# Up projection by Strassen's product, up and down as two stages

## The chip, the cores and the metric

One Trainium2 chip, one of its cores. The metric is device time of one execution in microseconds. The engines are named as in the profile: PE (TensorE; PEld are its weight loads), DVE (VectorE), ACT (ScalarE), POOL (GpSimd) and SP, which here only issues DMA transfers.

## What is computed

One decoder layer over 1024 tokens of width 1024 in float32: attention and a gated DeltaNet side by side, an MLP, a gated embedding and a last norm. The change is in the MLP:

```python
h = h + jnp.concatenate([attn_out, dn_out], axis=-1) @ w_o[i]
m = rmsnorm(h, norm_mlp[i])                                   # 1024 x 1024
h = h + jnp.square(jax.nn.relu(m @ w_up[i])) @ w_down[i]      # w_up 1024 x 4096, w_down 4096 x 1024
gate = jax.nn.sigmoid(rmsnorm(h, norm_ple[i]) @ w_ple_gate[i])
```

## The kernel before

Everything is kept transposed: channels lie on the 128 partitions, tokens in columns, in two halves `hb` of 512 tokens. `hT(hb, j)` is the piece of h for channels 128 j to 128 j + 127 and half hb.

Each float32 operand is split in two numbers of the PE's rounded type: `split` makes the high part on ACT (L219, a cast) and the low part on DVE or POOL (L220, source minus high part). `mm3` (L232) then takes three matmuls per product: high x high, high x low, low x high. A matmul has a 128x128 weight piece and 512 tokens.

The rows 1/rms of the norm don't enter the operand: `norm_M` makes M = h x gain alone (L1237 and L1238), `rows_M` squares and sums h, takes the power -0.5 on POOL (`rstd`, L1252), and spreads the row over all partitions by two matmuls with ones (`dg`, `row_bc`). The result `rB[hb]` multiplies the relu's argument when a bank of PSUM is read (`relu2`, L1288), ACT squares it (L1289), and it is split into `aT`.

The MLP is one loop over 8 values of c, 512 of the 4096 inner channels each. Up: two halves mp of 256 columns, four loads of weights each (`wunit2`: 2 k tiles x 256 columns, 256 KB), 8 k tiles, two token halves, two column pieces, three passes. Down, for the same c right behind it: two halves nh of 512 output columns, two token halves, 4 k tiles, 4 column pieces, three passes; the four banks are added to h by DVE (L1339). The first up products use banks and an order of their own, because the last group of w_out (`w_out(1)`, banks named bk_6732 and bk_6733 below) still runs then. After the loop come the gate weights `WG` and the last loop over token tiles.

The program is recorded in Python order, and a scheduler then fixes the order on every engine; each engine works through its own list in that order and waits at an instruction whose inputs are not there. Transfers of one queue are issued in order too. Tiles come from pools with a fixed number of buffers: `wraw` 2 (loaded weights), `wsp` 4 (split weights), `cvp` 2.

Of the kernel before, what the change touches and what calls it, by code (L numbers as in the profile page):

```python
# [18 lines left out]
P = 128  # L19
# [99 lines left out]
def hybrid_block(ctx, tc, t, out):  # L119
# [112 lines left out]
    def mm3(o, lh, rh, first, last):  # L232
        for i, (a, b) in enumerate(PASSES):
            T.matmul(o, lh(a), rh(b), start=first and i == 0, stop=last and i == 2)
# [996 lines left out]
    FIRST = (4, 5, 0, 1, 2, 3, 6, 7)  # L1231

    def norm_M(hb):

        for j in FIRST:
            h, g = hT(hb, j), gmlp[:, j:j + 1]
            A.activation(uview(M[hb], 0, j), h, AF.Copy, scale=g)  # L1237
            V.scalar_tensor_tensor(uview(M[hb], 1, j), h, g, uview(M[hb], 0, j).bitcast(F32),  # L1238
                                   op0=ALU.mult, op1=ALU.subtract)

    def rows_M(hb):
        for j in range(KT):
            x = cvp.tile([P, HB], F32, tag="cv", name=nm("sq")) if j else rB[hb]
# [3 lines left out]
        yield  # L1247
# [4 lines left out]
        G.tensor_tensor(r, r, mhalf[:, 0:4], op=ALU.pow)  # L1252
        yield
        b, dg = bank(ps["w"]), row_bc(r, aT[:, :, 3, HB:])
        yield
        for i in range(2):
            T.matmul(b, onesR, dg[:, i], start=i == 0, stop=i == 1)
        A.copy(rB[hb], b)

# [4 lines left out]
    psum(px, y=4, w=1)  # L1264
    zr, hn = part("Z"), part("AT0")
    rB.append(zr[:, 0:HB])
    with ahead(mark):
        norm_M(0)
        for _ in rows_M(0):
            pass  # L1270
    norm_M(1)

# [10 lines left out]
    def relu2(b, m, hb):  # L1283
        if m % 2:
            r = cvp.tile([P, 512], F32, tag="cv", name=nm("r"))
        else:
            r = zr[:, D + 512 * hb:D + 512 * hb + 512]
        V.scalar_tensor_tensor(r, b, 0.0, rB[hb], op0=ALU.max, op1=ALU.mult)  # L1288
        A.activation(r, r, AF.Square)  # L1289
        hi = aT[:, 0, m, hb * HB:(hb + 1) * HB]  # L1290
        lo = aT[:, 1, m, hb * HB:(hb + 1) * HB]
        split(hi, lo, r, G)

    def late(bs):

        yield from rows_M(1)
        for m in range(2):
            relu2(bs[m], m, 1)
        yield

    for c in range(FF // 512):
        for mp in range(2):
            bs = quad() if c else banks(("wyyy", "gggy")[mp])
            order = range(KT // 2) if c + mp else [k // 2 for k in FIRST[::2]]
            for i, k2 in enumerate(order):
                w = wunit2(t["w_up"], k2, c * 512 + mp * 256, G if k2 % 2 else V)
                if not c and mp:
                    for _ in range((0, 1, 2, 3).count(i)):
                        next(steps, None)
                for kk in range(2):  # L1310
                    kt = k2 * 2 + kk
                    for hb in range(2):
                        for m in range(2):
                            o = kk * 256 + m * P
                            mm3(bs[hb * 2 + m], lambda a: w[:, a, o:o + P],
                                lambda b: uview(M[hb], b, kt), i + kk == 0, i * 2 + kk == KT - 1)
            if c + mp == 0:
                rows_M(1)
            for hb in range(2):
                if c + mp == 0 and hb:  # L1320
                    steps = late(bs[2:])
                    continue
                for m in range(2):
                    relu2(bs[hb * 2 + m], mp * 2 + m, hb)
# [143 lines left out]
```

## Time and profile before

| | |
|---|---|
| median of 3 runs | 1398.19 us (1395.56 to 1399.04) |
| the profiled execution | 1398.71 us, its span 1396.90 us |
| TensorE clock granted, mean | 0.99 |
| PE busy | 1362.1 us, 98% |
| DVE, ACT, POOL busy | 664.4, 500.2, 492.8 us |

The span is from the first to the last instruction of the profiled execution. Busy time of PE is that of pipelined matmuls, so it says that PE had matmuls under way, not that it ran at its peak. The slices of the page cut the span in 40 pieces of 35 us; the MLP fills slices 17 to 37.

### The profile page before, as it was taken

How to read it: one execution, taken by the hardware profiler on the slowest of the kernel's cores; microseconds unless marked ns; L12 is line 12 of the kernel's file. 1: busy time of each engine (PE TensorE's matmuls, PEld its weight loads, DVE VectorE, ACT ScalarE, POOL GpSimd, SP SyncE). 2: the span in 40 equal slices, each digit the busy share in tenths (PEclk: the TensorE clock that was granted, in tenths of full speed). 3: DMA queues.
4: the chain of work that ended last, by engine and by line, in shares of the span. 5: the costliest groups of instructions: out<-in, count | busy, mean ns of one | idle time of the engine just before them, and what ended most of it. 6: DMA issues, size and time to landing. Idle time of an engine off the chain costs nothing.

```text
span 1396.9 us, 20219 instructions
## 1 busy us (share of the span) xinstructions
PE 1362.1 (98%) x7856; PEld 1159.6 (83%) x7856; DVE 664.4 (48%) x1312; ACT 500.2 (36%) x1030; POOL 492.8 (35%) x486
## 2 busy tenths in 40 slices
PE   8989999999997999999999999999999999999997
PEld 7788778999787998988888888888888888888886
DVE  6876967797376665533223132231312312145443
ACT  6455466534454343433031220312203122053333
POOL 6673636532484533333041320413204132040232
PEclk9999999999999998999999999999999999999999
DMA  6313222233146321221011210112101121043211
GB/s 212 98 46 77 54 60 51 73 78 88 34 140 197 108 71 54 91 76 46 23 53 46 69 45 31 53 46 68 46 24 61 46 64 49 24 128 120 84 46 46
DMA packets 85490, 98.68 MB, mean 71 GB/s; under 512 B 15281, under 2 KB 66529, under 8 KB 85393
## 3 DMA queue, kind: packets, MB, share of 16 engines
q1 hardware_dynamic: 82496, 91.63, 22.1%
q10 hardware_dynamic: 2544, 4.99, 1.1%
q8 instruction: 62, 1.02, 0.3%
q0 software_dynamic: 352, 0.76, 0.2%
q14 instruction: 36, 0.29, 0.1%
HBM read 87.90 MB, written 9.45 MB: 70 GB/s over the span
## 4 chain that ended last, share of the span: by engine, by line
PE 71%; DMA 2%; POOL 1%; DVE 1%; issue 1%; ACT 1%; SPq 0%; POOLq 0%; DVEq 0%; ACTq 0%
PE bk L102 69%; PE bk L106 1%; DMA PD<-po 1%; DMA raw<-in_w_proj 0%; DMA rD<-LD 0%; POOL w L220 0%; POOL cc L713 0%; POOL rk L706 0%; DVE Z L1387 0%; ACT oS L911 0%; POOL oss L942 0%; DVE oS L947 0%; POOL AT L220 0%; POOL R L220 0%; ACT Z L1390 0%
## 5 line engine op out<-in xcount | busy, mean ns | idle before, releaser
L220 POOL TENSOR_TENSOR w<-raw,w 128x512 fp32r<-128x512 f32 x144 | 190.8, 1326 | 533.4 <-ACT w L219 433.4
L219 ACT CAST w<-raw 128x512 fp32r<-128x512 f32 (+1 forms) x248 | 153.5, 619 | 570.4 <-PE bk L102 359.8
L102 PE MATMUL bk<-R,w 128*128 128x256 f32 (+1 forms) x1920 | 348.3, 330 | 3.9 <-ACT po L1070 3.9
L102 PE MATMUL bk<-aT,w 128*128 128x512 f32 x1536 | 349.8, 389 | 0.0
L102 PEld LDWEIGHTS bk<-aT,w 128*128 128x128 f32 x1536 | 288.3, 188 | 60.3
L102 PEld LDWEIGHTS bk<-R,w 128*128 128x128 f32 x1920 | 285.5, 190 | 39.9 <-ACT po L1070 4.1
L102 PE MATMUL bk<-M,w 128*128 128x512 f32 x768 | 198.8, 394 | 0.0
L220 DVE TENSOR_TENSOR w<-raw,w 128x512 fp32r<-128x512 f32 (+1 forms) x104 | 79.0, 759 | 242.0 <-ACT w L219 241.7
L102 PEld LDWEIGHTS bk<-M,w 128*128 128x128 f32 x768 | 144.3, 188 | 34.4
L1339 DVE TENSOR_TENSOR H<-bk,H 128x512 f32<-128x512 f32 x96 | 65.0, 690 | 107.1 <-PE bk L102 107.1
L220 POOL TENSOR_TENSOR aT<-Z,aT 128x512 fp32r<-128x512 f32 x32 | 41.6, 1299 | 139.0 <-ACT aT L219 139.0
L102 PE MATMUL bk<-U,w 128*128 128x512 f32 (+1 forms) x384 | 75.7, 344 | 0.0
L102 PE MATMUL bk<-w,U 128*128 128x256 f32 (+2 forms) x384 | 64.6, 321 | 7.3 <-DVE w L220 3.1
L102 PEld LDWEIGHTS bk<-U,w 128*128 128x128 f32 x384 | 58.9, 189 | 15.4 <-issue 7.3
L102 PE MATMUL bk<-w,R 128*128 128x256 f32 (+1 forms) x480 | 68.2, 292 | 0.1
L102 PEld LDWEIGHTS bk<-w,R 128*128 128x128 f32 x480 | 61.2, 192 | 7.6 <-issue 6.1
L102 PEld LDWEIGHTS bk<-w,U 128*128 128x128 f32 x384 | 55.7, 194 | 14.1 <-DVE w L220 3.3
L1339 DVE TENSOR_TENSOR AT<-bk,AT 128x512 f32<-128x512 f32 x32 | 21.9, 691 | 59.3 <-PE bk L102 59.3
L102 PE MATMUL bk<-M,aT 128*128 128x512 f32 (+1 forms) x204 | 47.9, 383 | 0.0
L102 PE MATMUL bk<-R,aT 128*128 128x512 f32 (+1 forms) x204 | 47.8, 383 | 0.0
L220 POOL TENSOR_TENSOR aT<-r,aT 128x512 fp32r<-128x512 f32 x32 | 45.1, 1410 | 0.7 <-ACT aT L219 0.7
L1288 DVE SCALAR_TENSOR_TENSOR Z<-bk,rsb 128x512 f32<-128x512 f32 x16 | 11.1, 691 | 70.8 <-PE bk L102 70.8
(336 smaller groups left out, 1769.3 us busy)
## 6 DMA issues: line engine op xcount, KB each, us to landing
raw<-in_w_in SPq DMA_DIRECT2D x72, 256.0 KB, 2.8
raw<-in_w_up SPq DMA_DIRECT2D x64, 256.0 KB, 2.7
raw<-in_w_down SPq DMA_DIRECT2D x64, 256.0 KB, 2.7
raw<-in_w_o SPq DMA_DIRECT2D x32, 256.0 KB, 2.9
PD<-po SPq DMA_DIRECT2D x16, 256.0 KB, 3.6
rawg<-in_w_gate SPq DMA_DIRECT2D x16, 256.0 KB, 2.8
pr<-PD SPq DMA_DIRECT2D x8, 512.0 KB, 3.3
AT<-in_xT SPq DMA_DIRECT2D x14, 256.0 KB, 4.5
```

The source lines that it names most:

```text
L102: self.tc.nc.tensor.matmul(o, lh, rh, **k)
L106: self.tc.nc.tensor.transpose(o, x, i)
L219: A.copy(hi, src)
L220: lo_eng.tensor_tensor(lo, src, hi.bitcast(F32), op=ALU.subtract)
L1288: V.scalar_tensor_tensor(r, b, 0.0, rB[hb], op0=ALU.max, op1=ALU.mult)
L1339: V.tensor_tensor(h, bs[m], h, op=ALU.add)
```

## The change

Up is computed for 16 groups n of 256 inner channels (class `Quad`). In a group, the even and the odd k tiles, the two column pieces f of 128 and the two token halves make a 2 x 2 by 2 x 2 block product, and that is done by seven products instead of eight (p1 to p7, each 4 k tiles x 3 passes = 12 matmuls). The weights' sums `S1`, `S2`, A11 - A21 and A12 - S2 are made by DVE for each group; the operands X1 to X7, sums of pieces of h x gain, once, by `half`, in eight buffers `T` of the pool `mt`, in `R1` (X5 and X3) and in `AT0` and `Z` (X4). p2 adds into the bank of p1, p7 into that of p6, p3 into that of p5; what has to be kept of the first one is read out in between (`s` by ACT, `U2` and the sum of L1374 by DVE). The banks' sums, relu and squares give four pieces, which ACT stores into DRAM tiles `AD[n]`.

The first four groups begin with p1 of all four and then p2 of all four, from weights loaded by `block`; these need only the first token half. The rest of X is prepared meanwhile.

Down runs behind all of up. It loads its activations from `AD` (two tiles per c; those of the first c into the last two weight buffers, `first`) and splits them in pieces of 128 x 1024 into `T` buffers. The pool `wdn` has five buffers instead of six, and the first down weights are put in `wsp`. The last stage takes `T` buffers where it had `M` and `aT`.

```diff
     px = ExitStack()
-    mt0p = px.enter_context(tc.tile_pool(name="mt0p", bufs=1))
-    atp2 = px.enter_context(tc.tile_pool(name="atp2", bufs=1))
-    wdn = px.enter_context(tc.tile_pool(name="wdn", bufs=6))
-    M = [mt0p.tile([P, 8192], F32R, tag="M0", name="M0"), R1]
-    aT = atp2.tile([P, 2, 4, S], F32R, tag="aT", name="aT")
-    rB = [rsb[1]]
+    mt = px.enter_context(tc.tile_pool(name="mt", bufs=8))
+    ux = ExitStack()
+    uw = ux.enter_context(tc.tile_pool(name="uw", bufs=1))
+    rB = [rsb[1], uw.tile([P, HB], F32, tag="rB", name="rB1")]
+    AD = [dram.tile([P, 2048], F32, tag=f"AD{n}", name=f"AD{n}") for n in range(16)]
...
+    def tmp(i):
+        p, tag, w, n = ((cvp, "cv", HB, None), (wraw, "raw", WN, None), (uw, "o", HB, 3), (uw, "s", HB, 2))[i]
+        return p.tile([P, w], F32, tag=tag, name=nm("t"), bufs=n)[:, :HB]
...
+    def half(i, p):
+        j, k = 2 * i, 2 * i + 1
...
+        o = tmp(2) if p > 3 else None
+        if p == 1:
+            scaled(1, i, hT(0, j), j)
+        elif p == 2:
+            scaled(2, i, hT(0, k), k)
+        elif p == 3:
+            scaled(3, i, hT(1, k), k)
+        elif p == 5:
+            V.tensor_tensor(o, hT(1, j), hT(0, j), op=ALU.subtract)
+            scaled(5, i, o, j)
+        else:
+            if p == 6:
+                V.tensor_tensor(o, hT(1, j), hT(0, j), op=ALU.subtract)
+                A.activation(o, o, AF.Copy, scale=gj)
+                V.scalar_tensor_tensor(o, hT(1, k), gk, o, op0=ALU.mult, op1=ALU.subtract)
+            elif p == 7:
+                A.activation(o, hT(1, j), AF.Copy, scale=gj)
+                V.scalar_tensor_tensor(o, hT(1, k), gk, o, op0=ALU.mult, op1=ALU.subtract)
+            else:
+                a, b = (cols(x, i).bitcast(F32) for x in X[6])
+                V.scalar_tensor_tensor(o, hT(0, k), gk, a, op0=ALU.mult, op1=ALU.subtract)
+                V.tensor_tensor(o, o, b, op=ALU.subtract)
+            split(hi, lo, o, V)
...
+        def product(self, p, b, src, eng):
+            first = p in (1, 6, 5, 4)
+            if first:
+                self.b[b] = bank(ps[("yyyy", "gggw")[self.n % 2][b]])
+            w = wsp.tile([P, 2, WN], F32R, tag="w", name=nm("w"))
+            w = w[:, :, :HB].rearrange("p b (i c) -> p b i c", i=4)
+            split(w[:, 0], w[:, 1], src, eng)
+            for i in range(4):
+                mm3(self.b[b], lambda a: w[:, a, i], lambda b: cols(X[p][b], i), first and i == 0, i == 3,
+                    skip_group_check=not first)
+        def put(self, r, f, hb, src=None):
+            V.scalar_tensor_tensor(r, r if src is None else src, 0.0, rB[hb], op0=ALU.max, op1=ALU.mult)
+            A.activation(r, r, AF.Square)
+            o = f * 1024 + hb * HB
+            A.dma_start(AD[self.n][:, o:o + HB], r)
...
+        def p5(self):
+            self.product(5, 2, self.S1, V)
+            r = tmp(1)
+            V.tensor_tensor(r, self.b[2], self.U3, op=ALU.add)
+            self.put(r, 1, 1)
...
+    r0, r1 = rows_M(0), rows_M(1)
+    for q, i in zip(qs, (0, 0, 3, 3)):
+        q.p1(q.block(0), i)
+        if q is qs[0] or q is qs[3]:
+            next(r0)
+    squares(1, 2)
+    for q in qs:
+        q.p2(q.block(1), V, 2)
+        if q is qs[2]:
+            next(r1)
...
+    for n in range(16):
+        q = qs[n].load() if n < 4 else Quad(n).load()
+        if n < 4:
+            q.p6()
+            if n == 0:
+                next(r1)
+                for p in (5, 4, 3):
+                    for i in range(4):
+                        half(i, p)
+        else:
+            q.p1()
+            q.p6()
+            q.p2()
+        for p in (q.p7, q.p5, q.p4, q.p3):
+            p()
+    first = []
+    for n in range(2):
+        raw = uw.tile([P, 8, 256], F32, tag="raw8", name=nm("raw8"), bufs=2).rearrange("p a c -> p (a c)")
+        SY.dma_start(raw, AD[n])
+        first.append(raw)
+    ux.close()
+    wdn = px.enter_context(tc.tile_pool(name="wdn", bufs=5))
...
     for c in range(FF // 512):
-        for mp in range(2):
...
+        aT = []
+        for f in range(4):
+            a = mpart()
+            if c:
+                raw = wdn.tile([P, S], F32, tag="ra", name=nm("ra"), bufs=2)
+                SY.dma_start(raw, AD[2 * c + f // 2][:, f % 2 * S:f % 2 * S + S])
+            else:
+                raw = first[f // 2][:, f % 2 * S:f % 2 * S + S]
+            split(a[:, :S], a[:, S:2 * S], raw, G if f % 2 and c else V)
+            aT.append(a)
```

Where instructions stand now. ACT's list at the start of up, before: `w_` are the casts of weights (w_6938 is up's first), `rh` that of the row rstd, R_75 the operands M of the second half, L1258 the copy of the spread row.

```order
L1237 ACTIVATE R_75<-AT_78,gmlp 128x512 x2
L1237 ACTIVATE R_75<-H,gmlp 128x512 x2
L219 CAST w_6938<-raw_6936 128x512
L1237 ACTIVATE R_75<-H,gmlp 128x512
L219 CAST rh_6908<-rstd 128x4
L1237 ACTIVATE R_75<-H,gmlp 128x512
L219 CAST w_6967<-raw_6965 128x512
L219 CAST w_6996<-raw_6994 128x512
L1258 COPY rsb<-bk_6907 128x512
```

The same place of ACT's list now: T_6876 and T_6878 are the high parts of X6 and X7, t_ their sums, bk_6964 the bank of p1 of group 0, w_6998 and w_7018 the weights of p1 of groups 1 and 2.

```order
L1276 ACTIVATE R_75<-AT_78,gmlp 128x512
L1352 COPY t_6980<-bk_6964 128x512
L219 CAST T_6876<-t_6940 128x512
L219 CAST T_6878<-t_6946 128x512
L1297 ACTIVATE t_6951<-t_6951,gmlp 128x512
L1300 ACTIVATE t_6957<-AT_78,gmlp 128x512
L219 CAST rh_6989<-rstd 128x4
L1243 ACTIVATE t_7060<-H 128x512
L219 CAST w_6998<-raw_6995 128x512
L219 CAST w_7018<-raw_7015 128x512
```

Before, rh stood between casts that PE needed later or had already; now the casts for PE's second and third product stand behind rh and behind operands made from w_out's last banks.

DVE's list at the end of w_out, before (L1022 adds a bank of w_out to h; bk_6732 and bk_6733 are the last two; L1251 is rstd, L220 the low parts):

```order
L1251 TENSOR_SCALAR rstd<-bk_6900 128x4
L220 TENSOR_TENSOR w_6938<-raw_6936,w_6938 128x512
L1238 SCALAR_TENSOR_TENSOR R_75<-H,gmlp,R_75 128x512
L220 TENSOR_TENSOR rh_6908<-rstd,rh_6908 128x4
L380 TENSOR_TENSOR aT<-con,rh_6908 128x512 x2
L1238 SCALAR_TENSOR_TENSOR R_75<-H,gmlp,R_75 128x512
L220 TENSOR_TENSOR w_6967<-raw_6965,w_6967 128x512
L1022 TENSOR_TENSOR AT_78<-bk_6732,AT_78 128x512
L1022 TENSOR_TENSOR AT_78<-bk_6733,AT_78 128x512
L1238 SCALAR_TENSOR_TENSOR R_75<-AT_78,gmlp,R_75 128x512 x2
```

And now, where bk_6744 and bk_6745 are the last two banks of w_out and T_6877, T_6879 the low parts of X6 and X7:

```order
L1022 TENSOR_TENSOR AT_78<-bk_6744,AT_78 128x512
L220 TENSOR_TENSOR T_6879<-t_6935,T_6878 128x512
L1022 TENSOR_TENSOR AT_78<-bk_6745,AT_78 128x512
L1298 SCALAR_TENSOR_TENSOR t_6940<-AT_78,gmlp,t_6940 128x512
L1301 SCALAR_TENSOR_TENSOR t_6946<-AT_78,gmlp,t_6946 128x512
L1296 TENSOR_TENSOR t_6951<-AT_78,H 128x512
L1277 SCALAR_TENSOR_TENSOR R_75<-AT_78,gmlp,R_75 128x512
L1251 TENSOR_SCALAR rstd<-bk_6982 128x4
L220 TENSOR_TENSOR T_6877<-t_6940,T_6876 128x512
L220 TENSOR_TENSOR T_6879<-t_6946,T_6878 128x512
L1298 SCALAR_TENSOR_TENSOR t_6951<-AT_78,gmlp,t_6951 128x512
L1301 SCALAR_TENSOR_TENSOR t_6957<-AT_78,gmlp,t_6957 128x512
```

rstd of the first half stood ahead of the additions of w_out's last two banks, and stands behind them now. Between the second of these additions and the sum U2 of group 1, which lets p7 of group 1 begin, there are now 75 more steps of DVE.

At the seam of up and down, a place that the program before does not have, DVE's list is now as follows. w_9317 are the weights of p3 of the last group, bk_9220, bk_9275 and bk_9296 the banks of its p6 and p7, of its p5 and of its p4, T_9352 and T_9355 activations of the first c, read from raw_9338, and w_9364 the first down weights.

```order
L220 TENSOR_TENSOR w_9317<-raw_9195,w_9317 128x512
L220 TENSOR_TENSOR T_9352<-raw_9338,T_9352 128x1024
L220 TENSOR_TENSOR T_9355<-raw_9338,T_9355 128x1024
L1369 TENSOR_TENSOR t_9273<-bk_9220,t_9216 128x512
L1374 TENSOR_TENSOR t_9291<-bk_9275,t_9273 128x512
L1344 SCALAR_TENSOR_TENSOR t_9291<-t_9291,rB_6512 128x512
L1379 TENSOR_TENSOR t_9273<-bk_9296,t_9273 128x512
L1344 SCALAR_TENSOR_TENSOR t_9273<-t_9273,rsb 128x512
L220 TENSOR_TENSOR w_9364<-raw_9362,w_9364 128x512
```

The sum of L1374, behind which PE may write p3 into bk_9275, stands behind both splits of activations. On ACT the casts of T_9352 and T_9355 stand in the same way ahead of the square and the store of t_9253, and t_9253 lies in the buffer that raw_9362 is loaded into.

## Rows read from the trace of the kernel before

**Rows 1.** The page: busy time of engines, and PE by slices.
```profile
PE 1362.1 (98%) x7856; PEld 1159.6 (83%) x7856; DVE 664.4 (48%) x1312; ACT 500.2 (36%) x1030; POOL 492.8 (35%) x486
...
PE   8989999999997999999999999999999999999997
```

**Rows 2.** The chain of waits: start, us, engine, what, of its longest link.
```profile
562.37 730.42 PE bk L102 x3287
```

**Rows 3.** Busy time by stretches (columns in line one): first down, both projections.
```profile
core 0: us, PE busy (x) PEld busy (x) DVE busy (x) ACT busy (x) POOL busy (x), PEclk, DMA share, GB/s
632.59:676.16 43.57, 43.57 (x193) 36.03 (x192) 14.63 (x23) 9.65 (x17) 11.46 (x9) 1.00 0.12 37
586.70:1292.60 705.90, 705.90 (x3084) 578.00 (x3083) 202.10 (x290) 167.42 (x289) 167.56 (x128) 1.00 0.18 56
```

**Rows 4.** Groups of DVE by line (busy us, mean ns), then one line's min/median/max.
```profile
L220 DVE TENSOR_TENSOR w<-raw,w 128x512 fp32r<-128x512 f32 x96 | 72.1, 751 | 238.5 <-ACT w L219 238.2
L1339 DVE TENSOR_TENSOR H<-bk,H 128x512 f32<-128x512 f32 x96 | 65.0, 690 | 107.1 <-PE bk L102 107.1
L1398 DVE SCALAR_TENSOR_TENSOR AT<-AT,ba,Z 128x1024 f32<-128x1024 f32 x7 | 9.0, 1284 | 4.6 <-POOL ba L1397 4.6
L1246 DVE TENSOR_TENSOR rsb<-rsb,sq 128x512 f32<-128x512 f32 x7 | 6.2, 888 | 3.5 <-ACT sq L1244 3.4
...
L1246 DVE TENSOR_TENSOR rsb<-rsb,sq x7: 675/832/1348, 468.1 to 523.8; 128x512 f32<-128x512 f32 x7
```

**Rows 5.** ACT and POOL by line; the last row is min/median/max ns.
```profile
L219 ACT CAST w<-raw 128x512 fp32r<-128x512 f32 x240 | 148.5, 619 | 568.5 <-PE bk L102 359.8 <-DMA raw<-in_w_down 80.3 <-DMA raw<-in_w_up 51.9
L1395 ACT ACTIVATE Z<-AT 128x1024 f32<-128x1024 f32 x7 | 7.4, 1060 | 7.5 <-POOL AT L1388 7.5
L220 POOL TENSOR_TENSOR w<-raw,w 128x512 fp32r<-128x512 f32 x144 | 190.8, 1326 | 533.4 <-ACT w L219 433.4 <-issue 93.5 <-DVE s L558 3.6
...
L1252 POOL TENSOR_TENSOR rstd<-rstd,mhalf x2: 1007/1196/1386, 579.2 to 626.3; 128x4 f32<-128x4 f32 x2
```

**Rows 6.** DMA: KB, median us to landing; then one line's issue and landing.
```profile
raw<-in_w_down SPq DMA_DIRECT2D x64, 256.0 KB, 2.7
PD<-po SPq DMA_DIRECT2D x16, 256.0 KB, 3.6
H<-in_xT ACTq DMA_DIRECT2D x3, 1024.0 KB, 6.9
...
L1004 ACTq DMA_DIRECT2D H<-in_xT x3: 380/388/582, 398.1 to 435.8; - x3
DMA to landing us min/median/max: 5.1/6.5/10.1
```

**Rows 7.** A wait of PE in order of time, then stretches (columns above).
```profile
446.91 4.14 PE L102 MATMUL bk<-R,w 128*128 128x256 f32 x20 [3.85 <-ACT po L1070]
...
443.00:446.90 3.90, 0.06 (x1) 0.00 (x0) 3.29 (x9) 1.24 (x3) 1.26 (x1) 1.00 0.84 271
446.90:449.00 2.10, 2.09 (x10) 2.09 (x11) 0.00 (x0) 2.10 (x5) 1.55 (x2) 0.50 0.56 177
449.00:451.00 2.00, 2.00 (x14) 2.00 (x13) 0.00 (x0) 0.17 (x1) 2.00 (x2) 0.67 0.29 80
```

**Rows 8.** PE in order of time, end of w_out (start us, us).
```profile
573.95 3.36 PE L102 MATMUL bk<-R,w 128*128 128x256 f32 x27
577.15 0.94 PE L102 MATMUL bk<-ones,rsb 128*128 128x1 f32 x8
577.96 2.74 PE L102 MATMUL bk<-R,w 128*128 128x256 f32 x21
...
583.97 0.40 PE L102 MATMUL bk<-aT,ones 128*128 128x512 f32 x1
584.20 0.52 PE L102 MATMUL bk<-AT,w 128*128 128x256 f32 x3
...
586.70 0.86 PE L102 MATMUL bk<-M,w 128*128 128x512 f32 x3
```

More of the change, by code (lines that the diff above doesn't have):

```diff
@@ L230, in hybrid_block, with mm3 @@
     PASSES = ((0, 0), (0, 1), (1, 0))
-    def mm3(o, lh, rh, first, last):
+    def mm3(o, lh, rh, first, last, **k):
         for i, (a, b) in enumerate(PASSES):
-            T.matmul(o, lh(a), rh(b), start=first and i == 0, stop=last and i == 2)
+            T.matmul(o, lh(a), rh(b), start=first and i == 0, stop=last and i == 2, **k)
     def mm3h(o, lh, rh, first, last):
@@ L1246, in rows_M @@
                 V.tensor_tensor(rB[hb], rB[hb], x, op=ALU.add)
-        yield
+    def rows_M(hb):
         b, r = bank(ps["w"]), rstd[:, hb * 4:hb * 4 + 4]
@@ L1252, in rows_M @@
         G.tensor_tensor(r, r, mhalf[:, 0:4], op=ALU.pow)
+        dg = row_bc(r)
         yield
-        b, dg = bank(ps["w"]), row_bc(r, aT[:, :, 3, HB:])
-        yield
+        b = bank(ps["w"])
         for i in range(2):
@@ L1258, in rows_M @@
         A.copy(rB[hb], b)
+        yield
     mark = tc.cur_priority
@@ L1264, in hybrid_block, with cols, scaled @@
     psum(px, y=4, w=1)
-    zr, hn = part("Z"), part("AT0")
[L1266 to L1271, printed above, removed]
+    def cols(x, i):
+        return x[:, i * HB:(i + 1) * HB]
+    X = {}
+    def scaled(p, i, x, j):
+        hi, lo = (cols(y, i) for y in X[p])
+        g = gmlp[:, j:j + 1]
+        A.activation(hi, x, AF.Copy, scale=g)
+        V.scalar_tensor_tensor(lo, x, g, hi.bitcast(F32), op0=ALU.mult, op1=ALU.subtract)
@@ new lines, in half @@
+    def half(i, p):
+        j, k = 2 * i, 2 * i + 1
+        gj, gk = gmlp[:, j:j + 1], gmlp[:, k:k + 1]
+        hi, lo = (cols(x, i) for x in X[p])
+        o = tmp(2) if p > 3 else None
[21 more added lines that the diff above has]
+            split(hi, lo, o, V)
@@ new lines, in hybrid_block @@
+    X[1], X[2], X[6], X[7] = ([mpart(), mpart()] for _ in range(4))
+    qs = [Quad(n) for n in range(4)]
+    with ahead(mark):
+        for i in range(4):
+            half(i, 1)
+        for i in range(4):
+            half(i, 2)
+        squares(0, 0)
+        for i in range(4):
+            half(i, 6)
+            half(i, 7)
+    r0, r1 = rows_M(0), rows_M(1)
[4 more added lines that the diff above has]
+    squares(1, 2)
@@ new lines, in hybrid_block @@
+    for q in qs:
+        q.p2(q.block(1), V, 2)
+        if q is qs[2]:
+            next(r1)
+    X[5] = [R1[:, 2048:4096], R1[:, 6144:8192]]
+    X[3] = [R1[:, 0:2048], R1[:, 4096:6144]]
+    X[4] = [part("AT0", F32R), part("Z", F32R)]
+    for n in range(16):
[5 more added lines that the diff above has]
+                for p in (5, 4, 3):
+                    for i in range(4):
+                        half(i, p)
[5 more added lines that the diff above has]
+            p()
@@ L1281, in quad @@
         return banks("gggw" if par[0] else "yyyy")
[L1283 to L1299, printed above, removed]
-    for c in range(FF // 512):
-        for mp in range(2):
[L1303 to L1324, printed above, removed]
+    for c in range(FF // 512):
+        aT = []
[8 more added lines that the diff above has]
+            aT.append(a)
         for nh in range(2):
@@ L1345, in hybrid_block @@
             i = kt * 2 + nh
-            o = (i % 8) * 1024
-            m = M[i // 8]
+            if i > 7 and i % 2 == 0:
+                wg = mpart()
+            m, o = (R1, i * 1024) if i < 8 else (wg, i % 2 * 1024)
             raw = wdn.tile([P, 512], F32, tag="rawg", name=nm("rawg"), bufs=2)
```

64 lines of the change are left out of this document (51 added, 13 removed).

## The prediction

> **What bounds the kernel now.** I read the page first: PE is busy for 1362.1 of 1396.9 us and no slice of the MLP falls below nine tenths; DVE has work for 48% [rows 1]. The chain of waits then says where the end is made: one link of 730.42 us, from 562.37 on, is PE alone, with no other engine in it [rows 2]. The table by stretches narrows it: from 586.70 to 1292.60, which is the up and down projections, PE is busy all 705.90 us at full clock, DVE for 202 and ACT for 167 us [rows 3]. So in this stage time is matmuls times their pace, and whatever takes matmuls away is gained as long as nothing else gets in front of PE. The pace: the first down half, 632.59 to 676.16, holds 192 matmuls of 512 columns (one of the 193 counted overlaps the edge), 43.57 us / 192 = 226.9 ns [rows 3].
>
> **What is taken away.** Up has 8 x 2 x 4 x 2 x 4 x 3 = 1536 matmuls; now 16 groups x 7 products x 12 = 1344. The lists agree: 192 fewer of 512 columns. 192 x 0.2269 = **-43.6 us**. Weights and moving operands keep their shape, so I see no reason for another pace; the bounds are 188 ns (PEld 36.03 us / 192, the weight load alone) and 226.9: -36 to -43.6.
> The Trainium skill would price this lower: its page "TensorE: Matmul & The Clock Gate" (section "Back-to-back issue gap") gives about 131 ns per matmul for a stream of 512 columns. By that figure the term would be 25.2 us, an estimate from the page. No stretch of this trace shows 131 ns; the row decides.
>
> **A middle group costs nothing.** Its seven products take 84 x 0.2269 = 19.06 us. DVE gets 18 steps in it (five splits, four weight sums, five additions out of PSUM, four relus): at 0.69 (the PSUM additions) 12.4 us, at 0.75 (the splits) 13.5 [rows 4]. ACT gets seven casts, four squares, one copy and four store issues: 12 x 0.62 + 4 x 0.39 = 9.0; POOL 2 x 1.33 = 2.7 [rows 5, 6]. All hide beneath PE. Three times per group a product follows another into its bank (p2 after p1, p7 after p6, p3 after p5), once ACT or DVE has read it. PE's list puts at least one other product, 2.72 us, between; the read costs 0.7. Uncovered, it would be 0.7 to 1.5 us each. DMA: 1 MB of weights in and 1 MB of activations out per 19.06 us is 110 GB/s, where 271 was moved in a worse place [rows 7]. In the down stage the splits of the activations move from 128x512 to 128x1024 pieces (ACT 1.06 us) [rows 5], the same columns in fewer steps; DVE has 2 x 1.28 + 20 x 0.69 = 16.4 us of work per 43.57. I take 0 for both, and 0 to +4 for the range.
>
> **The opening costs.** Before, preparing an operand meant one ACT and one DVE step per k tile, done under w_out. Now X6, X7 and later X5, X4, X3 are sums of both token halves, so most must wait for w_out's last banks. I lay the queues side by side on the clock of the trace. w_out's last group starts at 573.95 [rows 8]; the row sums (0.81) and two broadcasts (2 x 0.235) that ran inside it now stand behind it, so it ends at 586.70 - 0.81 - 0.47 = 585.4.
> (a) PE does p1 of group 0 (2.7) and row sums (0.8): 588.9. Its next matmul needs the cast w_6998. On ACT that stands behind the cast of rh (ACT's list), rh behind POOL's pow (1.2 [rows 5]), pow behind rstd on DVE. At 585.4 DVE is two steps behind, and rstd comes seven full steps from the first addition on (it is 0.15 itself): 9 x 0.69 + 0.2 brings it to 591.8, pow to 593.0, three ACT steps to 594.4. PE idles **5.5**.
> (b) The low half of that weight stands behind four more DVE steps: **1.5**. (c) The squares of half 1 share three buffers between ACT and DVE: **0.5**. (d) The second row sums repeat the chain, with less ahead of it: **2.5**.
> (e, f) From the end of p6 of group 0 to its partner's U2 sum, which frees p7 of group 1, DVE has 32 steps: 32 x 0.69 = 22.1 us, plus about 1 of waits. PE has six products to put there, 6 x 2.72 = 16.3. The rest is idle: **6**.
> Sum 16. Each step at half, since a scheduler's list may run better than a walk by hand: 8. With DVE at 0.89 instead of 0.69 (the sums that ran beside a busy POOL [rows 4]) over the 79 steps of (a) to (f): +16, of which I put 10 into the bound: 26.
>
> **The seam costs too.** Before, down of one c follows up of the same c and finds its activations in SBUF. Now p3 of the last group waits: on DVE the sum that empties its bank (L1374) stands three places behind T_9352, which needs the 1 MB load raw_9338; and that load needs the weight buffer that the split of w_9317 frees. Count from the end of p2 of group 15: split done at 1.7 (a relu and the split behind it, both on DVE); a load of 1 MB lands in 5.1 to 6.9 [rows 6], so at 7.7; ACT's cast of 1024 columns 1.06, two DVE splits of 1.28 each (for 128x1024 [rows 4]), two sums of 0.69: 12.7. PE has p5, p7 and p4, 8.2 us, to put there: **4.5** idle. Then the first w_down load waits for a store of activations out of the same buffer, which ACT can only issue after both T casts: landing + 2.1 + 0.9 + 3.2 (a 256 KB write: 2.7 to 3.6) + 2.7 + 0.6 is 1.4 past the end of p3; the second weight again 1.1. Together **7**; without the T splits ahead of the sum it would be 3, with slow loads 11.
>
> **The clock.** After its 3.85 us of waiting at 443 PE gets 0.50 of the clock, 1.2 GHz, for 2.1 us and 0.67 on average for the next 2.0: 1.7 us lost [rows 7]. Two waits of mine are as long, (a) and the seam: **+2** and **+1.5** (some of it hides in waits that follow).
>
> **Sum.** The profiled execution took 1398.71 (span 1396.90 + 1.8 around it), 0.5 above the median of the three runs, 1398.19. -43.6 + 16 + 7 + 3.5 = -17.1, so 1381.6 for a like execution, 1381 at the median.
>
> **Rivals.**
> A, the cover holds: the lists were laid so that work is interleaved, and PE's list in fact splits products into pieces to fill gaps. Opening at most 6, seam at most 3: 1361 to 1367. Against it: a list doesn't shorten the chain in (a). 0.13.
> B, my sum with its bounds: opening 8 to 26, seam 3 to 11: 1367 to 1392. 0.63.
> C, DVE becomes the bound of the stage: it does from 19.06 / 18 = 1.06 us per step on. Its splits average 0.75, single sums beside a busy POOL took up to 1.35 [rows 4]; POOL now has less to do. At 0.89 only opening and seam suffer: 1390 to 1399. 0.14.
> D, slower: the bank handovers. DVE and ACT work through their lists in order, so one late step (a split waiting for a weight buffer) stands ahead of the sum that frees a bank. 48 handovers; beyond the 26.5 us of stalls above, 17 us are left, so from 0.36 us each the gain is gone, and at the uncovered 1.0 us it is 1381 + 48 = 1429. For it: four weight buffers for seven products. Against: by a walk through one middle group each handover has 2 us to spare. 0.10.
> E, that the work doesn't fall: excluded by the count. That a matmul taken away gives back less than its 226.9 ns, since the stream overlaps them: by the weight load alone (188 ns) with my stalls 1389, which is inside the range. By the 131 ns of the Trainium skill's page on TensorE it would be 1399, no change; less than 0.01, as every stretch here shows 226.9.
>
> **Numbers.** 1381, range 1366 to 1394: it leaves out about half of A, the top of C and D. Runs spread by 0.25%, so 0.3% (4 us, 1394 to 1402) is what can be told from no change. Faster: A, B and two thirds of C, 0.85; within 0.3%: 0.07; slower: most of D, 0.08.
>
> **What would show it.** Right: 1344 matmuls with `T`, `R` and `AT`/`Z` operands at 227 ns in the up stage; about 19.1 us per group from the fifth on without PE waits; PE waiting some 16 us in all between the last w_out matmul and p7 of group 1, longest on ACT's w L219 behind rh; a wait on DVE (L1374) at p3 of the last group, and on ACT for raw<-in_w_down right behind; the granted clock at 0.50 after each of the two. Wrong: waits in every group (D), DVE near 9 tenths all through the stage (C), or no wait above 2 us at either end (A).

## The result and the profile after

The changed kernel takes 1378.3 us (median of four runs, 1376.6 to 1380.1), the kernel before 1396.9 on the same chip: ratio 0.9866, 95% interval 0.9844 to 0.9888. 18.6 us are gained of the 44.5 that the matmuls left out are worth. Here is the page's first part, beside [rows 1]:

```profile
PE 1323.3 (96%) x7664; PEld 1123.0 (82%) x7664; DVE 849.8 (62%) x1562; ACT 550.7 (40%) x1082; POOL 447.0 (33%) x432
```

There are 192 matmuls fewer (7856 to 7664), and DVE has 185 us more to do. The table by stretches shows all of up and down, the middle groups, and a piece of down (the columns are those of [rows 3]):

```profile
582.99:1270.97 687.98, 670.90 (x2903) 546.08 (x2902) 378.57 (x537) 216.59 (x339) 122.56 (x76) 0.99 0.33 107
700.00:900.00 200.00, 200.00 (x865) 162.04 (x864) 128.69 (x186) 74.11 (x123) 31.25 (x21) 1.00 0.33 110
1000.00:1200.00 200.00, 200.00 (x884) 165.60 (x883) 73.87 (x100) 42.55 (x57) 48.35 (x29) 1.00 0.31 95
```

Up and down took 705.90 us before, all of them busy [rows 3]; now 687.98, of which PE is busy for 670.90 and stands still for 17.08. From 700 to 900 no wait is left. The waits lie at the opening; PE in order of time, only the rows with a wait, which stands in brackets with what ended it:

```profile
593.33 2.07 PE L102 MATMUL bk<-T,w 128*128 128x512 f32 x4 [6.61 <-ACT w L219]
...
615.33 0.73 PE L102 MATMUL bk<-T,w 128*128 128x512 f32 x2 [2.09 <-ACT w L219]
...
623.97 4.58 PE L102 MATMUL bk<-T,w 128*128 128x512 f32 x12 [2.26 <-DVE t L1359]
...
643.64 0.73 PE L102 MATMUL bk<-AT,w 128*128 128x512 f32 x2 [2.88 <-POOL w L220]
...
673.82 5.34 PE L102 MATMUL bk<-R,w 128*128 128x512 f32 x22 [2.13 <-DVE w L220]
...
944.08 1.17 PE L102 MATMUL bk<-T,w 128*128 128x512 f32 x4 [0.65 <-ACT R L1484]
```

With one of 0.17 us the five at the opening make 16.1; the last is the only one from the seam on, which lies near 921. And the clock, by stretches:

```profile
586.72:590.31 3.59, 0.00 (x0) 0.00 (x0) 3.59 (x7) 2.85 (x5) 0.29 (x1) 1.00 0.00 0
590.31:597.14 6.83, 3.81 (x9) 3.04 (x10) 6.83 (x13) 4.68 (x9) 1.70 (x1) 0.50 0.15 41
624.45:627.86 3.41, 3.41 (x9) 2.64 (x9) 2.74 (x5) 1.45 (x2) 0.00 (x0) 0.50 0.48 159
644.93:648.34 3.41, 3.41 (x10) 2.64 (x9) 1.00 (x2) 0.00 (x0) 0.00 (x0) 0.50 0.00 0
```

Three times PE gets 1.2 in place of 2.4 GHz: in the midst of the wait of 6.61 us, 0.5 us behind the one of 2.26, and 1.3 behind the one of 2.88. It is busy there for 10.6 us and loses half of that, 5.3.

**Where the 18 us come from.** In the stretch of up and down 44.5 us of matmuls are left out (192 at the pace of up, below). Given back are 17.1 of waits, 5.3 of clock, 1.3 for row sums and broadcasts that stood under w_out before, and 2.9 of busy time that I can't put down to anything. That leaves 17.9. The two profiled executions differ by more, 22.1 us of span, for the stretch ahead of up ended 3.7 us earlier. 1.3 of that are those row sums and broadcasts; the rest goes with the clock before the change, 0.50 from 549.31 to 559.55, where the changed kernel's profile has no fall. That is no gain of the change: warm and rows_b (below) are the same program up to there and have the fall, and in the profiles of kernels that differ only behind this place the stretch ends between 581.5 and 589.5.

### The profile page after: what moved, and what is told of

The parts are those of the page before. It is cut to its first block, busy times and chain, and to the rows that moved or that the text cites. A ratio compares the mean times of both kernels' runs of the same rounds, so it can differ in the third digit from the quotient of the medians.

```text
span 1374.8 us, 20428 instructions
## 1 busy us (share of the span) xinstructions
PE 1323.3 (96%) x7664; PEld 1123.0 (82%) x7664; DVE 849.8 (62%) x1562; ACT 550.7 (40%) x1082; POOL 447.0 (33%) x432
## 4 chain that ended last, share of the span: by engine, by line
PE 59%; DVE 5%; DMA 4%; issue 3%; POOL 2%; ACT 1%; SPq 0%; POOLq 0%; DVEq 0%; ACTq 0%
PE bk L102 58%; PE bk L106 1%; DMA PD<-po 1%; POOL w L220 1%; DMA AD<-t 1%; DMA ra<-AD 1%; DMA raw<-in_w_up 1%; DMA raw<-in_w_proj 0%; DVE T L220 0%; DVE w L220 0%; DMA rD<-LD 0%; DMA raw<-in_w_o 0%; DVE S L1355 0%; ACT w L219 0%; DVE R L1277 0%
## 5 line engine op out<-in xcount | busy, mean ns | idle before, releaser
L102 PE MATMUL bk<-T,w 128*128 128x512 f32 x2304 | 538.9, 393 | 11.7 <-ACT w L219 8.7
L102 PEld LDWEIGHTS bk<-T,w 128*128 128x128 f32 x2304 | 434.2, 189 | 108.0 <-ACT w L219 9.1
L220 POOL TENSOR_TENSOR w<-raw,w 128x512 fp32r<-128x512 f32 x140 | 194.1, 1388 | 615.9 <-ACT w L219 435.9
L102 PE MATMUL bk<-R,w 128*128 128x256 f32 (+1 forms) x1536 | 242.6, 312 | 4.8 <-ACT po L1070 2.3
L102 PEld LDWEIGHTS bk<-R,w 128*128 128x128 f32 x1536 | 211.8, 189 | 25.7 <-DVE w L220 2.6
L220 DVE TENSOR_TENSOR w<-raw,w 128x512 fp32r<-128x512 f32 (+1 forms) x124 | 90.7, 731 | 84.7 <-ACT w L219 84.6
L102 PE MATMUL bk<-AT,w 128*128 128x256 f32 (+1 forms) x256 | 65.8, 345 | 3.5 <-POOL w L220 2.9
L1345 ACT ACTIVATE t<-t 128x512 f32<-128x512 f32 x64 | 40.5, 632 | 49.0 <-DVE t L1344 43.5
L102 PEld LDWEIGHTS bk<-AT,w 128*128 128x128 f32 x256 | 42.7, 191 | 10.9 <-POOL w L220 3.3
L220 POOL TENSOR_TENSOR T<-ra,T 128x1024 fp32r<-128x1024 f32 x14 | 33.6, 2401 | 50.2 <-ACT T L219 50.2
L102 PE MATMUL bk<-R,T 128*128 128x512 f32 (+1 forms) x204 | 48.6, 386 | 0.0
L102 PE MATMUL bk<-T,T 128*128 128x512 f32 (+1 forms) x204 | 47.0, 379 | 0.0
L102 PEld LDWEIGHTS bk<-T,T 128*128 128x128 f32 x204 | 36.8, 188 | 7.8
```

The lines of the kernel that those rows point to most:

```text
L102: self.tc.nc.tensor.matmul(o, lh, rh, **k)
L220: lo_eng.tensor_tensor(lo, src, hi.bitcast(F32), op=ALU.subtract)
```

## Experiments

The theory: the matmuls give what they are worth, two stages and the middle groups cost nothing, and the opening gives a third to a half back, through DVE and ACT, whose lists are worked off in order. Rivals: the split in two stages costs (C, D and the seam of the prediction); the loss is DVE's sheer load; the waits are only moved when one of them goes. Each ratio is to the kernel before on the same chip; the changed kernel has 0.9866. "Idle" is the stretch of up and down less PE's busy time in it.

| kernel | median us | ratio, 95% | up and down us, idle us |
|---|---|---|---|
| changed | 1378.3 | 0.9866 (0.9844 to 0.9888) | 687.98, 17.08 |
| late_rows | 1377.0 | 0.9848 (0.9826 to 0.9871) | 688.13, 15.95 |
| warm | 1374.0 | 0.9821 (0.9802 to 0.9841) | 683.05, 7.88 |
| aligned0 | 1380.3 | 0.9867 (0.9847 to 0.9887) | 689.97, 16.22 |
| pool_low | 1383.4 | 0.9878 (0.9858 to 0.9898) | 692.18, 18.61 |
| eight | 1411.8 | 1.0099 (1.0084 to 1.0113) | 721.59, 9.61 |
| no_cover | 1372.5 | 0.9820 (0.9807 to 0.9834) | 681.47, 12.27 |
| no_first | 1390.4 | 0.9947 (0.9935 to 0.9960) | 700.88, 27.59 |
| rows_apart | 1367.0 | 0.9780 (0.9766 to 0.9793) | 678.96, 9.32 |
| rows_b | 1365.6 | 0.9758 (0.9745 to 0.9771) | 675.89, 6.76 |
| rows_p4 | 1367.5 | 0.9772 (0.9759 to 0.9785) | 679.49, 9.60 |
| cover2_rows | 1376.3 | 0.9836 (0.9822 to 0.9849) | 684.15, 12.11 |
| no_cover_rows | 1376.2 | 0.9820 (0.9802 to 0.9838) | 684.73, 11.19 |

**The eight products (eight).** `Quad` gets one method in place of p1 to p7; X1 and X2 are the even and odd k tiles of the first half, X8 and X3 of the second.

```diff
...
+        def run(self):
+            bs = banks(("yyyy", "gggw")[self.n % 2])
...
+                        for hb in hbs:
+                            x = X[((1, 2), (8, 3))[hb][j]]
+                            for i in range(4):
+                                mm3(bs[f * 2 + hb], lambda a: w[:, a, i], lambda b: cols(x[b], i), j + i == 0, j * 4 + i == 7)
...
+            for hb in range(2):
+                for f in range(2):
+                    self.put(tmp(f), f, hb, bs[f * 2 + hb])
...
```

> Up is computed by the ordinary eight products of 12 matmuls per group in place of seven, without the sums of weights, operands and banks; the two stages, the activations in DRAM and the down stage stay as in the changed kernel. Theory (the gain is the 192 matmuls alone, and what is given back is the preparation of the seven products' operands at the opening; two stages by way of DRAM cost nothing): 192 x 0.2318 = 44.5 us more matmuls than the changed kernel, 12 to 16 us of PE waits and 3 to 7 us of low clock fewer at the opening: 1378 + 44.5 - 15 to 23 = 1400 to 1408, that is 0 to 10 us over the kernel before. Rival (a good part of the expected gain went into the split in two stages): 1412 or more, with PE waits between the groups or at the seam.

1411.8, above the range of the theory and at the edge of the rival's. PE's waits in it:

```profile
PE bk L102 <- ACT w L219: 9.3, 2, 7.2
PE bk L102 <- DVE H L1441: 0.3, 1, 0.3
```

No wait between groups; but besides one of 2.1 us in the opening 7.2 us at the seam. There the first load of w_down is issued only at 950.1, because its buffer in `wraw` holds a result that waits for its store:

```profile
SPq L225 <- DMA AD<-t: 3.9, 1, 3.9
```

That is the mechanism of my seam term, in a kernel that puts its last results otherwise. 9.6 us are idle; twice, behind 612 and 954, the clock is at 0.50, with PE busy for 2.9 and 4.6 us and half of that lost; and 1.3 are the row sums and broadcasts. That tells 14.6 of the 15.7 us over the stretch of before. So two stages by way of DRAM cost nothing between the groups; at the seam that hangs on the order. Product for product the seven are worth 33.6 us of stretch here, with their opening paid; but some 9.5 of these are the seam of eight itself.

**The seam (no_first).**

```diff
...
-            if c:
-                raw = wdn.tile([P, S], F32, tag="ra", name=nm("ra"), bufs=2)
-                SY.dma_start(raw, AD[2 * c + f // 2][:, f % 2 * S:f % 2 * S + S])
-            else:
-                raw = first[f // 2][:, f % 2 * S:f % 2 * S + S]
+            raw = wdn.tile([P, S], F32, tag="ra", name=nm("ra"), bufs=2)
+            SY.dma_start(raw, AD[2 * c + f // 2][:, f % 2 * S:f % 2 * S + S])
```

> The activations of the first c of down are no longer loaded ahead into the buffers of w_up, but into those of the pool wdn like all others, whose memory comes free only when the last group is through. Theory (the seam costs nothing because these loads and splits lie beneath the last group): now a load of 512 KB (4.0 us), a cast of 1.05 and a split of 1.23 lie behind the last stores: PE waits 6 to 10 us at the seam, clock falls after it, 1385 to 1391. Rival (the order of the queues at the seam leaves room enough either way): PE waits under 2 us, 1377 to 1380.

1390.4, as the theory said: one wait at the seam, a little longer than its 6 to 10 us, and the clock behind it (PE in order of time, then stretches):

```profile
930.82 9.55 PE L102 MATMUL bk<-T,w 128*128 128x512 f32 x28 [11.20 <-ACT T L219]
```
```profile
923.28:936.93 13.65, 6.12 (x14) 4.81 (x15) 5.83 (x6) 5.87 (x8) 2.55 (x2) 0.50 0.76 250
```

The early loads are worth 12 us; with them PE doesn't wait at 921, and for 0.65 us at 944.

**The first rows, issued later (late_rows).**

```diff
-        if q is qs[0] or q is qs[3]:
+        if q is qs[2] or q is qs[3]:
             next(r0)
```

> The row sums of the first token half and their broadcast are issued after p1 of the third group in place of the first, so that the casts of w for p1 of the second and third group stand ahead of rh on ACT. Theory (each of the waits in the opening is a cost of its own, the first one made by the chain rstd, pow, rh): PE's wait of 6.61 us after p1 of the first group falls below 2, the later waits (2.09, 2.26, 2.88, 2.13) stay, and the granted clock no longer falls at 601: 6 to 9 us less than the changed kernel's 1378.3, so 1370 to 1372. Rival (DVE has some 75 steps in front of p7 of the second group, and whatever PE gains early it waits later): the waits ahead of p7 of the first and second group and of p3 grow by what the first one loses, and the time is within 2 us of 1378.

1377.0, no difference that the intervals can tell. That is the rival's time, but not its mechanism, for the later waits hardly grew (2.57, 1.45, 2.89 and 2.13 us). The first wait stayed and went to another place (PE in order of time):

```profile
591.33 0.72 PE L102 MATMUL bk<-ones,rsb 128*128 128x1 f32 x6
597.91 0.77 PE L102 MATMUL bk<-dg,ones 128*128 128x512 f32 x1 [5.86 <-DVE dg L380]
```

The two broadcast matmuls now stand on PE right behind the row sums, ahead of products whose operands are ready. The chain from sums to `dg` is what lasts 6 us, and PE waits wherever its end stands in PE's list.

**The chain pulled apart (rows_apart, rows_b).** `row_bc` moves behind the first `yield` of `rows_M`, and the pieces are issued where nothing waits:

```diff
         G.tensor_tensor(r, r, mhalf[:, 0:4], op=ALU.pow)
-        dg = row_bc(r)
         yield
+        dg = row_bc(r)
...
-        if q is qs[0] or q is qs[3]:
+        if q is qs[1]:
             next(r0)
...
+        q.p2(q.block(1), V, 2, (r0,) if q is qs[0] else ())
...
```

> The chain of the row sums is pulled apart for both halves: sums and pow after p1 of the second group, rh and dg with the broadcast after p2 of the first group; for the second half sums and pow after p6 of the first group, the rest after its p7, which is moved up to stand right behind p6. So no broadcast stands ahead of products that don't need it, as it did where the sums alone were moved. Theory (PE's first wait is the chain, and DVE has room after 600, where it stood idle for 7 us): the wait of 6.61 us goes to below 2.5, that of 2.09 too, p6 of the first group starts 6 to 9 us earlier, and the time is 6 to 10 us less: 1368 to 1372. Rival (DVE's queue ahead of p5 and p4 of the first group sets the end of the opening, whatever comes before): the waits at p5 and p4 grow to 8 us and more, and the time is 1375 to 1379.

1367.0, 1 us under the theory's range, and no wait longer than 2.91 us: the theory, against the rival. rows_b leaves p7 of the first group where it was:

> As the kernel with four groups and chains apart, but p7 of the first group is not moved up; only the broadcast of the second half stands behind it. Theory (of the gain of 11 us the chains made all, the place of p7 nothing): 1366 to 1369, waits of 8 to 11 us in all at X5, X4 and p7. Rival (p7 moved up is what let PE run on): a wait of 2 us or more at p7 as in the changed kernel, 1369 to 1373.

1365.6, the fastest kernel of all, 34 us (2.4%) under the kernel before on its chip. Its longest waits in up and down:

```profile
PE bk L102 <- DVE dg L380: 2.5, 2, 1.9
PE bk L102 <- ACT w L219: 1.6, 3, 1.0
PE bk L102 <- issue: 0.9, 1, 0.9
PE bk L102 <- DVE w L220: 0.7, 1, 0.7
...
```

None is longer than 1.9 us. So the move of the two chains made the gain, and p7's place none. Nor is it DVE's sheer load: DVE is busy for 382.4 us of this stretch, in the changed kernel for 378.6. It is the order of the lists.

**A filled wait (warm).** The results of these 28 matmuls are thrown away.

```diff
...
+            if self.n == 1:
+                self.b[0] = bank(ps["g"])
+                for _ in range(28):
+                    T.matmul(self.b[0], X[1][0][:, 0:P], cols(X[1][0], 0), start=True, stop=True)
```

> 28 matmuls of 512 columns whose result is thrown away stand on PE between the row sums and p1 of the second group, 28 x 0.227 = 6.35 us of the 6.61 us that PE waits there; all else is as in the changed kernel. Theory (the clock falls because PE stood still): the granted clock stays at 1 from 583 to about 630, p1 and p2 of the next groups run at 0.23 us per matmul, and p2 of the third group ends about 3.4 us earlier (half of the 6.8 us that were spent at 0.50); as the weights and the operands wait for DVE later on, 1 to 3.4 us of it remain in the time, so 1375 to 1377. Rival (the fall at 601 has another cause, or later waits take it all): the fall stays at 601, or the time stays within 1 us of 1378.

1374.0. The waiting is the same, filled with useless work, and yet the stretch is 4.9 us shorter. By stretches, the place where the clock had fallen, and the next fall:

```profile
590.00:600.00 10.00, 9.96 (x43) 7.73 (x42) 9.29 (x18) 7.45 (x16) 1.99 (x1) 1.00 0.19 52
623.08:626.50 3.42, 3.37 (x8) 2.72 (x9) 3.38 (x6) 1.44 (x2) 0.00 (x0) 0.50 0.23 54
```

The first fall is gone, the later ones, behind waits that stayed, are not. So the first fall came of PE's standing still. Of the 4.9 us the clock explains 1.9; a wait of 2.13 us that shrank to 0.35 makes 1.8 more, and the wait of 0.65 us at 944, which is gone, 0.65. Why these two went no run shows.

**Groups ahead (no_cover, no_cover_rows, cover2_rows).** The list of groups ahead is emptied (no_cover, no_cover_rows) or cut to two (cover2_rows). In no_cover, whose edit this is, the rows of the first half go behind p1 of the first group and those of the second behind its p6; in the other two the chains are pulled apart as in rows_apart.

```diff
-    qs = [Quad(n) for n in range(4)]
...
     for n in range(16):
-        q = qs[n].load() if n < 4 else Quad(n).load()
...
+        q = Quad(n).load()
+        q.p1()
+        if n == 0:
+            next(r0)
+            next(r0)
+            squares(1, 2)
+        q.p6()
...
```

> No group begins ahead of the others: the first four groups run p1, p6, p2, p7, p5, p4, p3 in turn like all later ones, and the rows of both halves are issued after p1 and p6 of the first group. Theory (the opening's cost is work of DVE in front of the first p7, p5 and p4, and p1 and p2 of four groups, 8 x 2.78 us, lie on top of it as cover): of the six products that no longer lie ahead, 16.7 us, most turns into PE waits at p6, p5 and p4 of the first group, and the time is 1386 to 1396. Rival (the cover only fills PE while DVE is as late as ever, because its casts and splits of eight more weights and the three relus stand in the same queue): waits of PE 16 to 20 us as before, at other places, and 1376 to 1383.

1372.5: both wrong, it is faster than the changed kernel. Its waits (PE in order of time):

```profile
595.16 1.22 PE L102 MATMUL bk<-T,w 128*128 128x512 f32 x2 [6.36 <-ACT w L219]
603.12 1.25 PE L102 MATMUL bk<-ones,rB 128*128 128x1 f32 x8 [1.86 <-DVE rB L1245]
606.89 2.07 PE L102 MATMUL bk<-T,w 128*128 128x512 f32 x4 [2.52 <-ACT w L219]
...
```

The first wait is as long as with four groups ahead. In the changed kernel the second product of the cover stood itself behind the chain of rows, so the cover began when the hole was over. Then the cover should pay once the chain is out of its way:

> No group ahead, as in the kernel without cover, and the rows pulled apart as in the kernel where both chains are moved: sums after p6 of the first group, rh and broadcast after p2, those of the second half after p7. Theory (the four groups ahead were no use only because the first chain of rows stood in their midst; with the chains out of the way they hide the 6 us until X6 is there): here PE waits 6 to 7 us for p6 of the first group, nothing covers it, and the time is 1370 to 1374, 3 to 7 us over the kernel with four groups and chains apart, 1367. Rival (the groups ahead cost as much in DVE's and ACT's queues as they hide): 1364 to 1368.

> Two groups ahead in place of four, chains of rows apart. Theory (a group ahead is worth as much as it hides of the wait for X6, 6 us after the end of p1 of the first group; p1 and p2 of two groups, 11 us, are enough for that): 1364 to 1368, the same as with four groups or up to 3 us less, as four splits, two relus and two copies fewer stand ahead of X5 and X4. Rival (the later waits for X5 and X4, which 22 us of cover put off, come back): 1369 to 1374.

0.9820 without groups ahead and 0.9836 with two, against 0.9780 (rows_apart) and 0.9758 (rows_b) with four: with the chains apart four groups are worth 6 to 9 us against none; the theory of the first of the two had 3 to 7. Its mechanism is not shown, though. Both times lie above what either side expected, 1376.2 and 1376.3, and in no_cover_rows no wait of 6 to 7 us stands at p6: the longest wait is 2.44 us. Of the 8.8 us by which its stretch is longer than that of rows_b, half is idle time and half busy time, with the clock near 0.50 over 12.9 us of busy time where rows_b has 6.4. Without groups ahead, pulling the chains apart gains nothing (0.9820 both times); with the chains together, the groups ahead gain nothing (0.9866 against 0.9820). Each pays only with the other. That two would be enough was wrong; whether two are any better than none the intervals don't tell.

**DVE's load (pool_low, rows_p4).**

```diff
-            split(hi, lo, o, V)
+            split(hi, lo, o, G)
```

> The low parts of the operands X6, X7 and X4 (12 splits of 128x512) are made by POOL in place of DVE. Theory (PE's waits in the opening come from DVE's queue, some 75 steps of 0.69 us): DVE has 12 steps of 0.69 us less, 8.3 us, of which 8 lie ahead of p7 of the second group; a POOL step takes 1.3 us and beside DVE up to 1.8, and those of X6 and X7 end later than on DVE. The waits of 2.26 and 2.88 us at p7 of the first two groups go, and 2 to 5 us are gained: 1373 to 1376. Rival (the chain of each operand, and not the queue, is what PE waits for): the splits of X6 and X7 come later, p6 of the first group waits up to 3 us, and the time is 1378 to 1382.

0.9878, not told apart from 0.9866, and no gain. The wait at p4 shrank from 2.88 to 0.47 us, but the first wait grew from 6.61 to 10.26:

```profile
599.16 0.77 PE L102 MATMUL bk<-dg,ones 128*128 128x512 f32 x1 [10.26 <-DVE dg L380]
```

Groups of DVE from 585 to 600 show why, first pool_low, with what POOL does while these steps run (from 598.34 to 600.71), then the changed kernel:

```profile
L380 DVE TENSOR_TENSOR dg<-con,rh 128x512 fp32r<-128x512 f32 x2 | 2.4, 1222 | 0.0
```
```profile
597.14 3.02 POOL L220 TENSOR_TENSOR T<-t,T 128x512 fp32r<-128x512 f32 x2
```
```profile
L380 DVE TENSOR_TENSOR dg<-con,rh 128x512 fp32r<-128x512 f32 x2 | 1.3, 674 | 0.0
```

DVE's own steps of two inputs became 1.2 in place of 0.67 us long beside POOL, so that nothing was taken off it: in the stretch of up and down DVE is busy for 390.1 us, in the changed kernel for 378.6. The Trainium skill ("SBUF — State Buffer", section "Who interferes with whom") says that a DVE instruction with two SBUF inputs contends with a GpSimd instruction that reads SBUF. These rows agree (0.67 to 1.22 us).

```diff
-            self.product(4, 3, self.A22, G)
+            self.product(4, 3, self.A22, V if self.n < 2 else G)
```

> As the kernel with four groups and chains apart, but the low part of the weights of p4 is made by DVE in place of POOL for the first two groups; in the changed kernel that POOL step took 3.54 us beside a busy DVE and PE waited 2.88 us for it. Theory (with the chains apart p4 waits for X4 and no longer for its weights): no difference, 1367 within 1.5 us. Rival (a POOL step beside a busy DVE still costs): 1 to 3 us less, 1364 to 1366.

0.9772 against 0.9780: no difference, as the theory said.

**The pace (aligned0).**

The split weights are laid out anew, and taken by `wtile` wherever they are made.

```diff
+    def wtile(name, n=512):
+        w = wsp.tile([P, 1056], F32R, tag="w", name=name)
+        return w[:, :2 * n].rearrange("p (b n) -> p b n", b=2)
...
```

> Only the layout of the split weights in the buffers of wsp changes: the low part begins 512 elements behind the high part, as in the pool wdn, in place of 528. In the trace of the changed kernel matmuls of 512 columns take 231.8 ns each in the up stage and in the first half of the first down product, whose weights lie in wsp, and 226.7 from there on, where they lie in wdn. Theory (the distance of the two parts makes the difference): 226.7 ns in the up stage as well, (1344 + 96) x 5.1 ns = 7.3 us less there, time 1370 to 1372. Rival (it is the place of the pool or something else of the stage): 231.8 ns as before, time 1378 within 1.5 us.

No difference, and the pace of the middle groups is the old one (861 matmuls):

```profile
700.00:900.00 200.00, 200.00 (x861) 161.51 (x860) 126.93 (x184) 72.93 (x121) 31.33 (x20) 1.00 0.33 111
```

## Why the prediction was right, step by step

1381 was predicted, 1378.3 came. Of case B the opening (8 to 26) came, and rows_b shows that the order of the lists makes it; the seam (3 to 11) didn't come, there it was as in case A (at most 3). Single terms were off by more than the sum was, in both directions.

- **What is taken away**, 43.6: 192 matmuls left out, as counted. I had taken their price, 226.9 ns, from a down half, and wrote that every stretch shows it. Up runs at another pace, above my bounds, as a row of the kernel before shows (192 up matmuls of the second c):

```profile
676.16:720.66 44.50, 44.50 (x193) 36.06 (x192) 9.00 (x14) 11.31 (x20) 11.89 (x9) 1.00 0.19 60
```

  231.8 ns, so 44.5. The bound of 188 is out: the seven products' stream runs at 200 / 865 = 231 ns. The Trainium skill gives about 131 ns for a stream of weight loads and matmuls of 512 columns ("TensorE: Matmul & The Clock Gate", section "Back-to-back issue gap"). No run here shows that.
- **A middle group costs nothing**: right, no wait from 700 to 900 with DVE at 64%. That rules out C and D here; only at the opening did PE wait for DVE's and ACT's lists.
- **The opening**, 16: waits of 16.1. By parts: (a) 5.5, it was 6.61, and by the chain named: POOL's pow, 1.99 us long where I had 1.2, then the cast of rh, then that of w, for which PE waits (POOL and ACT in order of time):

```profile
590.02 1.99 POOL L1252 TENSOR_TENSOR rstd<-rstd,mhalf 128x4 f32<-128x4 f32 x1 [10.75 <-DVE rstd L1251]
...
592.04 0.19 ACT L219 CAST rh<-rstd 128x4 fp32r<-128x4 f32 x1 [0.75 <-POOL rstd L1252]
...
592.67 1.12 ACT L219 CAST w<-raw 128x512 fp32r<-128x512 f32 x2
```

  (b) and (c) together 2, nothing to be seen; (d) 2.5, it was 2.09. (e, f) 6, it was 7.4 (2.26, 0.17, 2.88 and 2.13), but the step failed: the wait that it names, of p7 of group 1 for its sum U2, didn't come. That sum (the second of L1359) ended at 645.3, and p7 of group 1 stands among the matmuls from 651.58 on, ahead of which PE didn't wait (DVE, then PE):

```profile
644.66 0.67 DVE L1359 TENSOR_TENSOR t<-bk,t 128x512 f32<-128x512 f32 x1
...
672.11 0.69 DVE L1369 TENSOR_TENSOR t<-bk,t 128x512 f32<-128x512 f32 x1 [2.62 <-DMA AD<-t]
```
```profile
651.58 5.73 PE L102 MATMUL bk<-T,w 128*128 128x512 f32 x24
```

  In its place PE waited 2.26 us for the U2 of group 0, 2.88 for POOL's low half of p4's weights, a step of 3.54 us, and 2.13 for a low half by DVE, which stood in DVE's list behind a sum that waited 2.62 us for a store. So the size came out right because errors cancelled, which is luck. What I missed is that the four groups ahead gain nothing as long as (a) stands in their midst: no_cover was faster.
- **The seam**, 7: wrong, PE waited for 0.65 us, and that only at 944. (By the figures given its second part begins with 1.8, not 1.4.) The step that failed is "that load needs the weight buffer that the split of w_9317 frees". SP's waits show what L1431, the load of raw_9336 and raw_9338, waited for, and DVE's list in order of time what came when:

```profile
SPq L1431 <- DVE T L220: 7.1, 1, 7.1
SPq L1431 <- DMA raw<-AD: 5.2, 1, 5.2
```
```profile
904.45 1.23 DVE L220 TENSOR_TENSOR T<-raw,T 128x1024 fp32r<-128x1024 f32 x1
...
910.72 0.69 DVE L220 TENSOR_TENSOR w<-raw,w 128x512 fp32r<-128x512 f32 x1
911.79 2.36 DVE L220 TENSOR_TENSOR T<-raw,T 128x1024 fp32r<-128x1024 f32 x2 [0.39 <-ACT T L219]
915.79 0.69 DVE L1369 TENSOR_TENSOR t<-bk,t 128x512 f32<-128x512 f32 x1 [1.63 <-PE bk L102]
916.51 0.69 DVE L1374 TENSOR_TENSOR t<-bk,t 128x512 f32<-128x512 f32 x1
```

  raw_9338 went into the buffer of raw_9336: its load waited for that of raw_9336 to land, and then for the second split of raw_9336, which ended at 905.7. It did not wait for the split of w_9317, which came at 910.72. So it was issued 5 us earlier than I had it. Both its splits were through at 914.2, 1.6 us before the next sum, for which DVE waited for PE, and the sum of L1374 came in time. Which buffer a load gets is to be read from what its queue waits for, not from the order of names. The second part of the seam (1.4 and 1.1 us for weights behind a store) didn't show either.
- **The clock**, 3.5: 5.3. After (a) as forecast; none at the seam, but two at the opening behind waits of 2.26 and 2.88 us, to which I had given no fall.

The seam and its clock were 7.9 us too much (8.5 less 0.65). Too little were the clock of the opening, by 3.3 (5.3 less 2), and busy time that nothing explains, by 2.9. With 0.9 at the pace and 2.4 ahead of up that is chance, the sum came out 5 us above the profiled run (1381.6 to 1376.6) and 3 above the median. That it came so near is in part luck.

## What to carry to other kernels

Price the work that is left out by a row of the same stage, and then look at the first and the last two groups: there the new operands are made, and there about half of the gain stayed (16.1 us of waits and 5.3 of clock, of 44.5). Work put ahead to cover a wait covers nothing if a short chain that nobody needs yet (rows, pow, broadcast) stands among it on any in-order list; issue its end where its result is used. Moving one end of such a chain is not enough: look where the wait goes.

## What the hardware showed that I had not expected

- Matmuls of 512 columns ran at 231.8 ns in up and 226.9 in down in the kernel before, and at 231 and 226 in the changed one (865 and 884 in 200 us), all at the same clock. The slower pace goes with weights in `wsp`: the first 96 matmuls of the changed kernel's down, whose weights lie there too, are slower than those behind them, whose weights lie in `wdn` (PE in order of time):

```profile
920.93 22.50 PE L102 MATMUL bk<-T,w 128*128 128x512 f32 x96
944.08 327.05 PE L102 MATMUL bk<-T,w 128*128 128x512 f32 x1440 [0.65 <-ACT R L1484]
```

  The distance between high and low part is not the cause (aligned0). The difference is worth 7 us in the up stage, and its cause stays open.
- The clock fell to 1.2 GHz behind waits of 2.3 and 2.9 us, too. The length of a wait doesn't tell it: behind the one of 2.09 at 613 to 615 the clock stayed at 2.4, behind one of 2.09 us in eight, which ended at 612.86, it fell, and in rows_b it fell twice, though no single wait there was longer than 1.9:

```profile
619.89:623.30 3.41, 3.41 (x9) 2.65 (x10) 3.41 (x6) 0.35 (x1) 0.00 (x0) 0.50 0.45 126
626.72:630.13 3.41, 2.94 (x7) 2.36 (x8) 3.41 (x6) 0.00 (x0) 0.00 (x0) 0.50 0.00 0
```
- DVE's steps of two inputs took nearly twice as long beside POOL (0.67 to 1.22 us).
